# First V weights loaded into eight tiles of their own and split during the last rows of the start stage; one Sin for both rope tables

## The chip, the cores and the metric

The kernel runs on one core of one Trainium2 chip. The metric is the device time of one execution in microseconds. The kernel before was timed in 3 runs, with a median of 1419.71 us (1411.23 to 1421.71); a fourth execution was recorded by the hardware profiler.

## The reference, cut to what matters

One encoder layer on 1024 tokens of width 1024, float32. An adaLN vector gives shift and scale; `h` is the normed and modulated input; one projection of `h` gives, among others, the queries, keys and values of eight heads of banded attention ("chunk attention") and a rotary key of the latent attention.

```python
mod = jnp.dot(jax.nn.silu(c), w_ada[l]) + b_ada[l]
h = modulate(rmsnorm(x, g_attn_norm[l]), sh_a, sc_a)
proj = jnp.dot(h, w_in[l])
q_lat, kv_lat, k_rope, ca_qkv = jnp.split(proj, split_pts, axis=-1)
...
ang = positions.astype(jnp.float32)[..., None] * inv     # rope
cos = jnp.cos(ang)[:, :, None, :]
sin = jnp.sin(ang)[:, :, None, :]
```

Behind it come two attentions, an output projection, and a gated MLP with a short causal convolution.

## The kernel before

Tokens are tiled in 8 blocks of 128, the model width in 8 rows of 128 (`ND`, index `d`). Every product is made of three matmuls: each operand is split into a high half (rounded to the matmul's type) and a low half (the rest), and `gemm3` (lines 153 to 155) adds high by high (L153), high by low of the weight (L154) and low of the activation by high (L155). A weight tile is split in two steps: a copy that rounds (`hi_of`, L76 on ScalarE or L80 on VectorE) and a subtraction (`lo_of`, L83, mostly on POOL).

*The start stage* runs over `d` = 0 to 7. For each row, VectorE accumulates the adaLN vector from streamed weights (`adacc`, L254 and L256, tiles `adaw` in a ring of five), TensorE makes 8 transposes of `x` (`ht_ps`, L230), ScalarE and VectorE scale them (L233, L236, L238), POOL subtracts the low half of the first 512 tokens and VectorE that of the other 512 (both L239, tiles `hT`), and TensorE adds 24 matmuls to the first query/key product (`qk`).

*Behind the rows* the first V weights `wv0` are loaded by `load_w`: 8 tiles of 128 by 256 floats (128 KB each), in a ring of three raw tiles (`wr`) that all weights of this stage share. VectorE takes a sum of squares of each (L191, by `jt`) and rounds it (L80), POOL subtracts (L83). A block that is opened with `issue_after(x)` puts its instructions behind `x` on `x`'s engine; here the block stands behind the last low halves on VectorE and on POOL.

*Then the attention stage* begins. `f_v(0)` is the first of a list of "fillers": its products (`ipv`, 24 matmuls for 128 tokens) go through two PSUM banks (`mm`). 16 steps of the fillers, 96 matmuls, stand ahead of the first attention tile; then pages of queries and keys are transposed (`q_ps`, `k_ps`, L674) and score tiles (`sc`, L740) follow, with filler matmuls between them at a set ratio. `pow2_scale` (L298 to L310) makes a scale for V from the sums of squares, over one small matmul (`vspc`, L300). `qk_norm` norms queries and keys (L325 to L332, with a power on POOL, L117). The next weights, `wq1` and later `wq2`, come through the same ring `wr`; the bias tiles of the first heads (L852, masked on VectorE in L857 and L858) and all weights are issued by one queue, SyncE's (SP). The softmax is an Exp on ScalarE (L772) with a negative row minimum from VectorE (L761); its result is split (L72, L794) and transposed by DMA (L805).

The rope tables are a chain of small VectorE operations (`rope_tables`) that is woven into the attention stage; it ends with two Sin (L548 for the sine, L549 for the cosine), and four products each for two tables (L556). [...]

A scheduler puts each engine's instructions in order when the program is built, from the order in the source, the priorities and its own estimate of times; each engine then works through its list in that order.

Of the kernel before, what the change touches and what calls it, by code (L numbers as in the profile page):

```python
# [12 lines left out]
F32 = mybir.dt.float32  # L13
F32R = mybir.dt.float32r
# [3 lines left out]
AF = mybir.ActivationFunctionType  # L18
# [3 lines left out]
MUL, ADD, SUB, MIN, MAX = ALU.mult, ALU.add, ALU.subtract, ALU.min, ALU.max  # L22

P = 128
# [3 lines left out]
ND = D // P  # L28
# [35 lines left out]
def layer_kernel(ctx, tc, I, out):  # L64
    nc = tc.nc
    pe, act, dve, pool, sp = nc.tensor, nc.scalar, nc.vector, nc.gpsimd, nc.sync
# [7 lines left out]
    def hi_of(eng, o, i):  # L74
        if eng == "a":
            act.activation(o, i, AF.Copy)  # L76
        elif eng == "p":
            pool.tensor_scalar(o, i, 1.0, 0.0, op0=MUL, op1=ADD)
        else:
            dve.tensor_copy(o, i)  # L80

    def lo_of(eng, o, i, hi):
        (pool if eng == "p" else dve).tensor_tensor(o, i, f32(hi), op=SUB)  # L83
# [39 lines left out]
    hw = right.__enter__()  # L123
# [9 lines left out]
    st = startp.__enter__()  # L133
# [13 lines left out]
    anchor = {}  # L147
# [23 lines left out]
            yield 3 * len(part) * max(107, w / 2.4 + 2.5)  # L171


    def load_w(name, src, ncol, he="a", ssw=None, jt=None):
        tiles = []
        for k in range(ND):
            if ncol <= 256:
                w = hw.tile([P, 2, 256], F32R, name=f"{name}s{k}", tag="ws", bufs=16)
                hi, lo = w[:, 0, :ncol], w[:, 1, :ncol]
            else:  # L180
                wh = hw.tile([P, 512], F32R, name=f"{name}h{k}", tag="ws", bufs=16)
                wl = hw.tile([P, 512], F32R, name=f"{name}l{k}", tag="ws", bufs=16)
                hi, lo = wh[:, :ncol], wl[:, :ncol]
            for c0 in range(0, ncol, 256):
                c = slice(c0, min(c0 + 256, ncol))
                raw = hw.tile([P, 256], F32, name=f"{name}r{k}_{c0}", tag="wr", bufs=3)
                rw = raw[:, :c.stop - c0]
                anchor["sp"] = sp.dma_start(rw, src[:, k, c]).ins
                if jt:
                    junk = jt(f"{name}j{k}")[:, :c.stop - c0]  # L190
                    dve.tensor_tensor_reduce(junk, rw, rw, 1.0, 0.0, MUL, ADD, accum_out=ssw[:, k:k + 1])  # L191
                elif ssw is not None:
                    junk = qtile(f"{name}j{k}")
                    act.activation(junk[:, :c.stop - c0], rw, AF.Square, accum_out=ssw[:, k:k + 1])
                hi_of(he, hi[:, c], rw)
                lo_of("p", lo[:, c], rw, hi[:, c])
            tiles.append((hi, lo))
        return tiles
# [4 lines left out]

    def load_ada(dd, c):
        w = st.tile([P, 2, 512], F32, name=f"adaw_{dd}_{c}", tag="wa", bufs=5)
        sp.dma_start(w[:], I["w_ada_a"][dd][:, 2 * c:2 * c + 2])
        wada[dd, c] = w

    for c in range(4):
# [8 lines left out]
    for t in range(NT):  # L218
        xt = xs[t]
        junk = st.tile([P, D], mybir.dt.bfloat16, name=f"xj{t}", tag="hv", bufs=2)  # L220
# [25 lines left out]
    accs = {}  # L246
    ssw0 = cst.tile([P, ND], F32, name="ssw0")

    def ada_pair(dd):
        acc = rtile(f"adacc_{dd}")  # L250
        for k in range(ND):
            w = wada[dd, k // 2][:, k % 2]
            if k == 0:
                dve.tensor_scalar(acc[:], w, cs[:, 0:1], None, op0=MUL)  # L254
            else:
                dve.scalar_tensor_tensor(acc[:], w, cs[:, k:k + 1], acc[:], op0=MUL, op1=ADD)  # L256
        accs[dd] = acc

    ada_pair(0)
    for d in range(ND):  # L260
        dd, half = divmod(d, 2)
        if half == 0 and dd + 1 < ND // 2:
            for c in range(4):
                load_ada(dd + 1, c)
            ada_pair(dd + 1)
        pt = ps.tile([P, 512], F32, name=f"p_ada{d}", tag="mm", bufs=2)
        for i in range(2):
            c0 = half * 256 + i * P
            pe.matmul(pt[:, i:i + 1], accs[dd][:, c0:c0 + P], ones[:, 0:1], start=True, stop=True)

        tmp = cst.tile([P, 1], F32, name=f"adat{d}", tag="adat", bufs=2)
        dve.tensor_scalar(tmp[:], pt[:, 0:1], pk[:, C_B + 8 + d:C_B + 9 + d], 1.0, op0=ADD, op1=ADD)
        dve.tensor_tensor(modT[:, 0, d:d + 1], tmp[:], pk[:, C_GA + d:C_GA + d + 1], op=MUL)
        dve.tensor_tensor(modT[:, 1, d:d + 1], pt[:, 1:2], pk[:, C_B + d:C_B + d + 1], op=ADD)
        for h in range(2):
            hT[d, h] = mod_transpose(lambda j: xs[4 * h + j][:, d * P:(d + 1) * P], d, h, 0, ps, ("T", "pv")[h], 1,
                                     hw, "hT", st, 16, "v" if h else "a", "v" if h else "p")
        for t in range(NT):
            h, j = divmod(t, 4)
            sl = slice(j * P, (j + 1) * P)  # L280
            gemm3(qk0[h][:, j * 256:(j + 1) * 256],
                  [(hT[d, h][:, 0, sl], hT[d, h][:, 1, sl]) + wqk[d]], start=(d == 0 and j % 2 == 0), stop=(d == ND - 1 and j % 2 == 1))


    with tc.issue_after(anchor["lov"]), tc.issue_after(anchor["lop"]):
        wv0 = load_w("wv0_", I["w_v"][0], 256, he="v", ssw=ssw0,
                     jt=lambda n: st.tile([P, 512], F32, name=n, tag="hv", bufs=2))
    startp.__exit__(None, None, None)
    att = tc.tile_pool(name="att", bufs=1, side="left", reuse_waits="tile")
    at = att.__enter__()  # L290
# [192 lines left out]
    def rope_tables():  # L483
        cnt = [0]

        buf = [pgtile([P, 8, NT, 16], F32, f"rt{i}") for i in range(2)]

        def T():
            n = cnt[0] % 14
            cnt[0] += 1  # L490
            return buf[n // 8][:, n % 8]

        keep = (buf[1][:, 6], buf[1][:, 7])

        def rnd(src, q, o=None):
            o = T() if o is None else o
            dve.tensor_scalar(o, src, q, MAGIC, op0=MUL, op1=ADD)
            dve.tensor_scalar(o, o, MAGIC, None, op0=SUB)
            return o

        def fma(n, c, b):
            o = T()
            dve.scalar_tensor_tensor(o, n, c, b, op0=MUL, op1=ADD)
            return o

        p1 = _grid(TWO_PI, 2.0 ** -9)
        p2 = _grid(TWO_PI - p1, 2.0 ** -21)
        p3 = TWO_PI - p1 - p2

        def reduce(src):  # L510
            n = rnd(src, 1.0 / TWO_PI)
            yield
            r = fma(n, -p1, src)
            r = fma(n, -p2, r)
            yield
            return fma(n, -p3, r)

        pf = cst.tile([P, NT], F32, name="pf")
        dve.tensor_copy(pf[:], pos_i[:])
        ang = T()  # L520
        dve.tensor_tensor(ang, pf[:].unsqueeze(2).to_broadcast([P, NT, 16]),
                          pk[:, C_INV:C_INV + 16].unsqueeze(1).to_broadcast([P, NT, 16]), op=MUL)
        nh = rnd(ang, 2.0 ** -20, keep[0])
        rem = fma(nh, -(2.0 ** 20), ang)
        nm = rnd(rem, 2.0 ** -8, keep[1])
        lo = fma(nm, -(2.0 ** 8), rem)
        yield
        tot = yield from reduce(lo)
        for n, w in ((nh, 2.0 ** 20), (nm, 2.0 ** 8)):
            c = w - round(w / TWO_PI) * TWO_PI  # L530
            c1 = _grid(c, 2.0 ** -9)
            x = T()
            dve.tensor_scalar(x, n, c1, None, op0=MUL)
            yield
            x = fma(n, c - c1, (yield from reduce(x)))
            yield
            y = T()
            dve.tensor_tensor(y, tot, x, op=ADD)
            tot = y
        tot = yield from reduce(tot)  # L540
        yield
        pi_s = 3.1415925
        sn, cn, cl, c2, cl2 = T(), T(), T(), T(), T()
        dve.tensor_scalar(cl, tot, pi_s, -pi_s, op0=MIN, op1=MAX)
        dve.tensor_scalar(c2, tot, math.pi / 2, None, op0=ADD)
        yield
        dve.tensor_scalar(cl2, (yield from reduce(c2)), pi_s, -pi_s, op0=MIN, op1=MAX)
        act.activation(sn, cl, AF.Sin)  # L548
        act.activation(cn, cl2, AF.Sin)  # L549
        yield  # L550

        for tab, c0 in ((tabq, C_RQ), (tabk, C_RK)):
            for half, trig in ((0, cn), (1, sn)):
                for j in range(2):
                    o = half * 32 + j * 16
                    dve.tensor_tensor(tab[:, :, o:o + 16], trig,  # L556
                                      pk[:, c0 + j * 16:c0 + j * 16 + 16].unsqueeze(1)
                                      .to_broadcast([P, NT, 16]), op=MUL)
                    yield
# [285 lines left out]
    cnt = [0]  # L845
# [647 lines left out]
```

## Time and profile before

| | |
|---|---|
| runs | 1411.23, 1419.71, 1421.71 us; median 1419.71 |
| profiled execution | 1410.1 us; span of its trace 1408.3 us; mean granted TensorE clock 0.931 |
| busy in the span | TensorE 88%, VectorE 78%, POOL 50%, ScalarE 44% |
| chain that ended last | VectorE 35%, TensorE 30%, issue 10%, DMA 9%, POOL 8%, ScalarE 7% |

A row of the timeline gives start and duration in microseconds, the engine, the line, the operation, the tiles as out<-in, the count of merged instructions, and in brackets the idle time ahead of it with what ended it. A row of a group gives, after the bar, busy time and the mean nanoseconds of one. A row of waits gives total, number and longest. A row of the table by stretches gives for each engine busy microseconds and instructions, then the granted clock, the share of the DMA engines and GB/s. PE is TensorE, PEld its weight loads, DVE VectorE, ACT ScalarE, SPq the queue of SyncE.

### The profile page before, as it was taken

To read this page: it belongs to the slowest core of one execution; us is meant where nothing else is said; L and a number is where in the kernel's file an instruction comes from. 1 tells how busy PE (TensorE), PEld (TensorE's weight loads), DVE (VectorE), ACT (ScalarE), POOL (GpSimd) and SP (SyncE) were. 2 spreads that over 40 slices of the span, in tenths; PEclk is the share of its full clock that TensorE was granted. 3 is DMA by queue.
4 is the path that set the end of the run, shared out by engine and by line. 5 is a ranking of instruction groups with operands and counts; after the bars stand their busy time and mean duration, and the time that the engine had idled before them with its cause. 6 is when DMAs were issued, how large, how long until landed. Compare 5 with 4: busy or idle time off the path is not lost.

```text
span 1408.3 us, 18699 instructions
## 1 busy us (share of the span) xinstructions
PE 1234.5 (88%) x6156; PEld 1006.3 (71%) x6156; DVE 1093.0 (78%) x1861; ACT 624.0 (44%) x1132; POOL 709.3 (50%) x685
## 2 busy tenths in 40 slices
PE   4879688989777789995677999999999999999998
PEld 3868476978655567774565887787778777888886
DVE  6847879686579997882577888988888888698667
ACT  4433545444456554652274444344434444443331
POOL 5353366375545674443563677677667874200000
PEclk9989798998888889997887999999999999999999
DMA  8223567755221478877721323333232223894451
GB/s 314 93 64 79 132 149 177 169 134 106 57 53 42 88 169 178 164 160 230 279 90 45 113 95 123 127 119 127 91 108 89 101 99 118 303 350 130 125 163 60
DMA packets 223689, 190.56 MB, mean 135 GB/s; under 512 B 148709, under 2 KB 166885, under 8 KB 223593
## 3 DMA queue, kind: packets, MB, share of 16 engines
q1 hardware_dynamic: 223592, 189.38, 47.3%
q8 instruction: 48, 0.79, 0.2%
q14 instruction: 49, 0.39, 0.1%
HBM read 117.24 MB, written 37.49 MB: 110 GB/s over the span
## 4 chain that ended last, share of the span: by engine, by line
DVE 35%; PE 30%; issue 10%; DMA 9%; POOL 8%; ACT 7%; SPq 1%; POOLq 0%; DVEq 0%; ACTq 0%
DVE u L1157 5%; DVE u L1156 4%; PE dnA_P L1304 2%; PE dnA_P L1305 2%; PE dnA_P L1306 2%; ACT u L1155 2%; DVE hlc L794 2%; PE dnB_P L1306 1%; PE dnB_P L1305 1%; PE dnB_P L1304 1%; DVE hlm L794 1%; DMA wor<-w_out 1%; DMA aw<-w_ada 1%; PE sc L740 1%; PE sm L746 1%
## 5 line engine op out<-in xcount | busy, mean ns | idle before, releaser
L76 ACT ACTIVATE dnP<-dnr 128x1024 fp32r<-128x1024 f32 x73 | 77.3, 1062 | 111.8 <-PE dnA_P L1306 43.1
L1278 DVE TENSOR_TENSOR dnP<-dnr,dnP 128x1024 fp32r<-128x1024 f32 x72 | 90.3, 1259 | 44.9 <-ACT dnP L76 43.3
L1156 DVE SCALAR_TENSOR_TENSOR u<-c,cvp,u 128x1023 f32<-128x1023 f32 x44 | 81.9, 1902 | 46.3 <-ACT u L1155 46.3
L72 POOL TENSOR_SCALAR hlm<-Pm,rim 128x512 f16<-128x512 f32 (+2 forms) x96 | 69.8, 736 | 71.8 <-DVE rim L775 28.7
L1157 DVE SCALAR_TENSOR_TENSOR u<-c,cvp,u 128x1022 f32<-128x1022 f32 x44 | 86.5, 2003 | 0.0
L72 POOL TENSOR_SCALAR hlc<-Pc,ric 128x640 f16<-128x640 f32 (+2 forms) x64 | 47.1, 738 | 71.1 <-DVE ric L775 35.4
L794 DVE SCALAR_TENSOR_TENSOR hlm<-Pm,rim,hlm 128x512 f16<-128x512 f32 (+2 forms) x96 | 65.0, 688 | 6.2 <-POOL hlm L72 5.9
L772 ACT ACTIVATE Pc<-sc,mc 128x640 f32<-128x640 f32 (+2 forms) x64 | 42.1, 658 | 54.5 <-DVE mc L761 38.9
L772 ACT ACTIVATE Pm<-sm,mm 128x128 f32<-128x128 f32 (+3 forms) x64 | 47.1, 737 | 32.0 <-DVE mm L765 18.6
L794 DVE SCALAR_TENSOR_TENSOR hlc<-Pc,ric,hlc 128x640 f16<-128x640 f32 (+2 forms) x64 | 53.0, 830 | 10.0 <-POOL hlc L72 9.3
L76 ACT ACTIVATE wc<-ws 128x512 fp32r<-128x512 f32 x22 | 13.9, 633 | 103.1 <-DVE ws L1082 103.1
L1155 ACT ACTIVATE u<-c,cvp 128x1024 f32<-128x1024 f32 x44 | 52.1, 1234 | 13.5 <-DVE c L1228 6.8
L153 PE MATMUL ipq<-wq_s,hT 128*128 128x256 f32 x192 | 56.2, 296 | 1.2 <-ACT wq_s L76 1.2
L154 PE MATMUL ipq<-wq_s,hT 128*128 128x256 f32 x192 | 56.0, 292 | 0.6 <-POOL wq_s L83 0.6
L155 PE MATMUL ipq<-wq_s,hT 128*128 128x256 f32 x192 | 56.1, 292 | 0.0
L833 PE MATMUL pvm<-PTm,vt 128*128 128x256 f16 (+1 forms) x320 | 43.2, 284 | 12.6 <-DMA PTm<-hlm 8.8
L1232 ACT ACTIVATE u<-u 128x1024 f32<-128x1024 f32 x22 | 23.3, 1061 | 67.9 <-DVE u L1157 67.9
L83 POOL TENSOR_TENSOR wc<-ws,wc 128x512 fp32r<-128x512 f32 x22 | 34.3, 1558 | 36.4 <-ACT wc L76 36.4
L1306 PE MATMUL dnA_P<-dnP 128*128 128x512 f32 x132 | 51.4, 389 | 0.0
L1305 PE MATMUL dnA_P<-dnP 128*128 128x512 f32 x132 | 51.4, 389 | 0.0
L1304 PE MATMUL dnA_P<-dnP 128*128 128x512 f32 x132 | 51.2, 389 | 0.0
L83 POOL TENSOR_TENSOR wd<-wu,wd 128x512 fp32r<-128x512 f32 x22 | 30.4, 1382 | 37.5 <-ACT wd L76 37.5
(421 smaller groups left out, 4544.6 us busy)
## 6 DMA issues: line engine op xcount, KB each, us to landing
wu<-w_up SPq DMA_DIRECT2D x44, 512.0 KB, 3.5
dnr<-g_d SPq DMA_DIRECT2D x73, 256.0 KB, 4.3
aw<-w_ada SPq DMA_DIRECT2D x48, 256.0 KB, 3.5
g_d<-u SPq DMA_DIRECT2D x22, 512.0 KB, 2.8
dnr<-w_down SPq DMA_DIRECT2D x44, 256.0 KB, 5.4
adaw<-w_ada_a SPq DMA_DIRECT2D x16, 512.0 KB, 4.9
x<-x SPq DMA_DIRECT2D x16, 512.0 KB, 8.5
g_d<-gs SPq DMA_DIRECT2D x22, 256.0 KB, 2.0
```

What stands on the lines that cost most here:

```text
L72: pool.tensor_scalar(o, i, s, 1.0, op0=MUL, op1=MUL)
L76: act.activation(o, i, AF.Copy)
L83: (pool if eng == "p" else dve).tensor_tensor(o, i, f32(hi), op=SUB)
L772: act.activation(pr[:, :n], sv, AF.Exp, bias=m[:], scale=-1.0, accum_out=rsum[:, 0:1])
L794: dve.scalar_tensor_tensor(hl[:, w:2 * w], pp, ri[:], hl[:, :w], op0=MUL, op1=SUB)
L1155: act.activation(u[:], c, AF.Identity, scale=cvp[:, cv + 2:cv + 3], bias=cvp[:, cv + 3:cv + 4])
L1156: dve.scalar_tensor_tensor(u[:, 1:], c[:, :S - 1], cvp[:, cv + 1:cv + 2], u[:, 1:], op0=MUL, op1=ADD)
L1157: dve.scalar_tensor_tensor(u[:, 2:], c[:, :S - 2], cvp[:, cv:cv + 1], u[:, 2:], op0=MUL, op1=ADD)
L1278: r = f(*a, **k)
L1304: pe.matmul(pt, sh, w[:, 0, 0], start=start, stop=False, skip_group_check=add)
L1305: pe.matmul(pt, sh, w[:, 1, 0], start=False, stop=False, skip_group_check=add)
L1306: pe.matmul(pt, sl, w[:, 0, 0], start=False, stop=stop, skip_group_check=add)
```

## The change

First, `wv0` no longer goes through `load_w`. Eight raw tiles of their own (`wvr`, 8 buffers) are loaded right behind the last `adaw` load on SyncE's queue. They are split two at a time behind the low halves of rows 4, 5, 6 and 7: VectorE rounds and then sums squares, POOL subtracts. Second, the two Sin become one over 256 columns, whose two inputs lie side by side; the ring of small tiles in the chain shrinks from 14 to 10 for that.

```diff
-    def load_w(name, src, ncol, he="a", ssw=None, jt=None):
+    def load_w(name, src, ncol, he="a", ssw=None):
...
-                if jt:
-                    junk = jt(f"{name}j{k}")[:, :c.stop - c0]
-                    dve.tensor_tensor_reduce(junk, rw, rw, 1.0, 0.0, MUL, ADD, accum_out=ssw[:, k:k + 1])
-                elif ssw is not None:
+                if ssw is not None:
...
-        sp.dma_start(w[:], I["w_ada_a"][dd][:, 2 * c:2 * c + 2])
+        anchor["ada"] = sp.dma_start(w[:], I["w_ada_a"][dd][:, 2 * c:2 * c + 2]).ins
...
+    wv0, wv0r = [], []
+
+    def wv0_load():
+        with tc.issue_after(anchor["ada"]):
+            for k in range(ND):
+                r = st.tile([P, 256], F32, name=f"wv0_r{k}", tag="wvr", bufs=8)
+                anchor["sp"] = sp.dma_start(r[:], I["w_v"][0][:, k, :]).ins
+                wv0r.append(r)
+
+    def wv0_split(k):
+        w = hw.tile([P, 2, 256], F32R, name=f"wv0_s{k}", tag="ws", bufs=16)
+        junk = st.tile([P, 512], F32, name=f"wv0_j{k}", tag="wvj", bufs=1)
+        with tc.issue_after(anchor["lov"]), tc.issue_after(anchor["lop"]):
+            hi_of("v", w[:, 0], wv0r[k][:])
+            lo_of("p", w[:, 1], wv0r[k][:], w[:, 0])
+            dve.tensor_tensor_reduce(junk[:, :256], wv0r[k][:], wv0r[k][:], 1.0, 0.0, MUL, ADD,
+                                     accum_out=ssw0[:, k:k + 1])
+        wv0.append((w[:, 0], w[:, 1]))
...
             for c in range(4):
                 load_ada(dd + 1, c)
+            if dd + 2 == ND // 2:
+                wv0_load()
             ada_pair(dd + 1)
...
+        if d >= ND // 2:
+            for k in range(2 * d - ND, 2 * d - ND + 2):
+                wv0_split(k)
         for t in range(NT):
...
-    with tc.issue_after(anchor["lov"]), tc.issue_after(anchor["lop"]):
-        wv0 = load_w("wv0_", I["w_v"][0], 256, he="v", ssw=ssw0,
-                     jt=lambda n: st.tile([P, 512], F32, name=n, tag="hv", bufs=2))
...
-            n = cnt[0] % 14
+            n = cnt[0] % 10
...
-        sn, cn, cl, c2, cl2 = T(), T(), T(), T(), T()
+        cl, cl2, sn, cn, c2 = buf[1][:, 2], buf[1][:, 3], buf[1][:, 4], buf[1][:, 5], T()
...
-        act.activation(sn, cl, AF.Sin)
-        act.activation(cn, cl2, AF.Sin)
+        act.activation(buf[1][:, 4:6], buf[1][:, 2:4], AF.Sin)
```

## The prediction

> **What bounds the kernel now.** I read the table by stretches first, then the waits, then the queue and the engines in the stretch that stands out. The page says TensorE is 88% busy in a span of 1408.3 us, but the share is uneven.
>
> ```profile
> 56.00:68.00 12.00, 12.00 (x103) 11.99 (x103) 7.45 (x21) 6.30 (x10) 3.43 (x5) 1.00 0.01 2
> 68.00:93.20 25.20, 17.47 (x100) 15.49 (x99) 12.43 (x42) 6.72 (x15) 19.74 (x25) 0.73 0.28 86
> 101.20:140.00 38.80, 37.63 (x276) 33.64 (x277) 28.91 (x102) 17.28 (x38) 12.90 (x18) 1.00 0.32 72
> ```
>
> The last rows of the start stage fill TensorE (12.00 of 12.00 us). Then come 25.2 us with only 100 matmuls at a granted clock of 0.73, and after 101.2 TensorE is full again (37.63 of 38.80). The hole is the first V product.
>
> ```profile
> PE ipv L154 <- POOL wv_s L83: 4.2, 3, 3.5
> PE ipv L153 <- DVE wv_s L80: 1.5, 1, 1.5
> PE vspc L300 <- DVE vsc L298: 1.4, 1, 1.4
> ```
> ```profile
> SPq L188 <- POOL wv_s L83: 30.8, 4, 21.6
> ```
> ```profile
> 39.20 1.92 SPq L206 DMA_DIRECT2D adaw<-w_ada_a  x2
> 43.59 33.73 SPq L188 DMA_DIRECT2D wv_r<-w_v  x7
> 77.37 0.90 SPq L852 DMA_DIRECT2D bias<-bias  x2
> 78.37 15.33 SPq L188 DMA_DIRECT2D wq_r<-w_qk  x11
> ```
>
> TensorE waits for both halves of the V weights. The cause is the ring of three raw tiles: SyncE stands 21.6 us in one wait until POOL has released a tile, so seven loads of 128 KB take 33.73 us, and the biases and `wq1` queue behind them. TensorE's own rows give the pace:
>
> ```profile
> 65.19 0.40 PE L155 MATMUL qk<-wq_s,hT 128*128 128x256 f32 x2
> 68.00 0.28 PE L153 MATMUL ipv<-wv_s,hT 128*128 128x256 f32 x1
> 71.73 0.39 PE L153 MATMUL ipv<-wv_s,hT 128*128 128x256 f32 x1 [1.52 <-DVE wv_s L80]
> 75.61 0.58 PE L154 MATMUL ipv<-wv_s,hT 128*128 128x256 f32 x1 [3.49 <-POOL wv_s L83]
> 80.79 0.59 PE L300 MATMUL vspc<-vsc,ones 128*128 128x8 f32 x2 [1.41 <-DVE vsc L298]
> 81.82 0.58 PE L153 MATMUL ipv<-wv_s,hT 128*128 128x256 f32 x1 [0.43 <-DVE vsc L301]
> 93.00 0.28 PE L154 MATMUL ipv<-wv_s,hT 128*128 128x256 f32 x1
> 93.12 0.28 PE L155 MATMUL ipv<-wv_s,hT 128*128 128x256 f32 x1
> 101.20 0.30 PE L740 MATMUL sc<-k,qh 128*128 128x128 f32 x1 [1.64 <-DVE k L705]
> ```
>
> The 96 matmuls run from 68.00 to 93.24. Undisturbed they start every 0.12 us (the rows at 93.00 and 93.12), 11.5 us in all. The first score follows the last of them by 8 us.
>
> **The change part by part.** *The wait for V's weights.* With eight tiles nothing holds the loads back. The row at 39.20 shows the last `adaw` issued by 41.1; the queue row at 77.37 has 0.45 us for each 128 KB issue, so eight take 3.6 us and two biases 0.9, issued by 46. The first split stands behind row 4's low half, after 55, so the loads are hidden by 9 us of other work. The stretch of 25.2 us becomes 11.5 plus the handover at `vspc` (80.79 to 81.82, 1.0 us), which stays because it holds a PSUM bank of the pair. Gain: 25.2 - 12.5 = 12.7 us.
>
> *The splits, moved.* They now share rows 4 to 7 with work that TensorE waits for.
>
> ```profile
> 54.79 1.30 POOL L239 TENSOR_TENSOR hT<-hv,hT 128x512 fp32r<-128x512 f32 x1 [1.08 <-ACT hv L236]
> 62.76 1.32 POOL L239 TENSOR_TENSOR hT<-hv,hT 128x512 fp32r<-128x512 f32 x1 [2.42 <-ACT hv L236]
> ```
> ```profile
> 55.01 1.62 DVE L239 TENSOR_TENSOR hT<-hv,hT 128x512 fp32r<-128x512 f32 x1
> 61.38 0.81 DVE L238 TENSOR_SCALAR hv<-ht_ps,modT 128x512 f32<-128x512 f32 x1 [2.20 <-ACT hT L233]
> 62.22 0.69 DVE L239 TENSOR_TENSOR hT<-hv,hT 128x512 fp32r<-128x512 f32 x1
> ```
> ```profile
> L83 POOL TENSOR_TENSOR wv_s<-wv_r,wv_s 128x256 fp32r<-128x256 f32 x8 | 6.6, 846 | 3.4 <-DVE wv_s L80 3.2
> L117 POOL TENSOR_TENSOR r<-ss,nhalf 128x8 f32<-128x8 f32 x4 | 6.5, 1642 | 0.1
> L83 POOL TENSOR_TENSOR wq_s<-wq_r,wq_s 128x256 fp32r<-128x256 f32 x8 | 5.9, 734 | 3.7 <-ACT wq_s L76 3.7
> L191 DVE CUSTOM_DVE_ANT_0 wv_j<-wv_r 128x256 f32<-128x256 f32 x8 | 4.3, 548 | 3.0 <-DMA wv_r<-w_v 3.0
> L80 DVE CAST wv_s<-wv_r 128x256 fp32r<-128x256 f32 x8 | 2.7, 355 | 0.0
> L857 DVE TENSOR_SCALAR bias<-bias,pk 128x256 f32<-128x256 f32 x2 | 0.7, 346 | 0.0
> ```
>
> VectorE gets 2 x (0.36 + 0.55) = 1.8 us in a row and has 2.2 idle (61.38): it fits. POOL is tighter. In the built program its list has the subtractions of tiles 3, 4 and 5 ahead of row 7's low half, and tiles 4 and 5 are rounded on VectorE only behind row 6's low half there, which ended at 62.22 + 0.69 = 62.9. Round, square, round (0.36 + 0.55 + 0.36), then 0.73 on POOL: row 7's low half starts at 64.9 instead of 62.76, 2.1 late. It ended at 64.1 and TensorE used it at about 65.3 (second of the two at 65.19), so 1.2 us cover it and 0.9 shows. Row 6 has the same shape: 0.9 again. I take 2.0 with a little for the engines slowing each other. Bounds: 0 if idle time holds all, and 8 x 0.73 = 5.9 if every subtraction shows.
>
> [...] The row at 55.01 shows VectorE's subtraction at 1.62 us while POOL subtracts, against 0.69 alone. [...]
>
> *Bias masks.* VectorE's list has both masks (2 x 0.35, and two small fills) ahead of row 4's scaling, so 0.7 us or a little more is added there, and if the biases landed late VectorE would stand. They are issued by 46 and needed after 51. Behind VectorE wait the last `adacc` and TensorE's `p_ada`. I take 0.4; bounds 0 and 0.9.
>
> *The second ring.* What is late next is `wq1`, still in three tiles.
>
> ```profile
> 92.11 0.42 ACT L76 ACTIVATE wq_s<-wq_r 128x256 fp32r<-128x256 f32 x1 [1.07 <-DMA wq_r<-w_qk]
> 92.43 0.46 ACT L371 ACTIVATE v<-ipv,vabc 128x256 f16<-128x256 f32 x1
> ```
> ```profile
> 89.57 2.51 DMA wq_r<-w_qk
> 154.40 1.28 ACT L772
> 168.04 1.28 ACT L772
> 181.16 4.41 DMA wq_r<-w_qk
> 186.96 3.37 DMA aw<-w_ada
> ```
>
> The chain ran through this ring up to 92, just as TensorE finished: ScalarE evicts V behind the last `wq1` split. The new list on ScalarE has V's evictions between the splits of tiles 4, 5, 6 and 7, and POOL reaches `wq1` about 12 us earlier, behind three of the 1.64 us powers. One trip of the ring is 2.51 + 0.42 + 0.73 = 3.7 us. TensorE would finish near 82.9; I reckon two trips after POOL's third `wq1` subtraction near 79, so it is close: I take 0.5, bounds 0 and one trip, 3.7.
>
> *The Sin.* Two set loads and one Sin go.
>
> ```profile
> 150.81 1.28 ACT L548 ACT_TABLE_LOAD   x1
> 152.11 0.31 ACT L548 ACTIVATE rt<-rt 128x128 f32<-128x128 f32 x1
> ```
>
> The load ahead of Exp at 154.40 stands on the chain with 1.28 us; the one at 150.81 is covered by VectorE. I take -1.3; bounds 0 and -2.6 (both loads). [...]
>
> *The order behind it.* The scheduler also moved things in the lists from about 105 to 600 us, with the same instructions. No row prices that. The nearest are the two transfers on the chain at 181.16 and 186.96, 7.8 us, where weights stood behind other transfers on SyncE. I take 0 and 7.8 to either side.
>
> Sum: -12.7 + 2.0 + 0.4 + 0.5 - 1.3 + 0 = **-11.1 us**. Against the profiled execution's own 1410.1 that is 1399.0; against the median of the runs, 1419.71, it is 1408.6. The four executions form two pairs ten microseconds apart (1410.1 and 1411.2; 1419.7 and 1421.7), and a median of a few can fall into either, so I set the saving against their mean, 1415.7: **1404.6 us**.
>
> **The rivals.** *The ring takes the wait.* V's evictions wait on ScalarE for two more trips of `wq1` (7.4 us): -12.7 + 2.4 + 7.4 - 1.3 = -4.2, 1411.5. For it: the chain runs through just this ring now. Against it: the lists interleave. *The ports.* Every one of the eight VectorE squares meets a POOL subtraction and each meeting costs the 0.93 us of row 55.01, 7.4 in place of 2.0: -5.7, 1410.0. Against it: VectorE has 2.2 us idle in a row. *The new order helps.* `wq2`'s fourth to sixth tile are now issued in one go on SyncE; if the 7.8 us of the chain at 181 to 190 go, -18.9, 1396.8. *The new order hurts, and it ends slower.* Place: SyncE's list, where weights now stand ahead of the softmax transposes that TensorE's value products need; while a weight waits for its ring, the transposes behind it stand. Price: 7.8 us each time, as above. One such leaves -3.3; from the second on the kernel is slower (-11.1 + 15.6 = +4.5, 1420.2), and three give +12.3, 1428.0. Against it: POOL's list has the subtractions that free those tiles early. *The change doesn't do what it says:* biases or weights land late and VectorE stands in row 4; about 0, 1415.
>
> **How the numbers follow.** Forecast 0.52, order helps 0.17, ring 0.11, ports 0.08, order hurts 0.09, no effect 0.03. The extremes of all bounds are -12.7 - 2.6 - 7.8 = -23.1 (1392.6) and -12.7 + 5.9 + 0.9 + 3.7 + 7.8 = +5.6 (1421.3); runs in one pair or the other move this by some 5 us. The range is 1391 to 1422. One per cent, 14.2 us, is about what a measurement of this kernel can tell from no change. Faster by more than that: most of "order helps" and a quarter of the forecast case, 0.28. Slower by more: half of "order hurts" and a little of the unknown, 0.08. Within: 0.64.
>
> **What would show it.** Right: eight V loads issued between 41 and 46; no wait of TensorE on `wv_s`; about 13 us instead of 25.2 from the first `ipv` to the 96th, at a clock near 1.00; the first score near 91; one Sin of 256 columns with two set loads around it. Row 6 or 7 wrong: TensorE waits for POOL's `hT` by more than 2 us in all. Ring: ScalarE's V copies stand behind `wq_s` waiting for DMA and the first score is after 95. Order: the gain at 101.2 shrinks or grows between 105 and 600. The prediction is wrong if the first score comes early and the end does not.

## The result, and the profile after

The changed kernel takes 1406.3 us (median of 20 runs, 1399.0 to 1412.2) against 1414.45 us of the kernel before (20 runs, 1408.14 to 1427.44). The ratio is 0.9941, 95% interval 0.9925 to 0.9958; by the ratio that is 8.3 us less. Run again beside the later experiments it gave 0.9941 once more (0.9922 to 0.9961). The profiled execution after, 1412.2 us, is the longest of its runs, and the one before, 1410.1, is among the shortest of its own; so the two traces are compared stage by stage and not by their ends, and each kernel has a second trace (after 1404.9 us, before 1415.2).

The table by stretches of the first trace after (columns as in the prediction's):

```profile
56.00:68.00 12.00, 11.17 (x90) 10.31 (x88) 11.93 (x32) 5.13 (x7) 6.86 (x8) 1.00 0.01 2
68.00:93.20 25.20, 20.57 (x148) 20.27 (x149) 14.45 (x31) 9.54 (x22) 18.82 (x23) 0.87 0.14 43
```

The hole has shrunk: 148 matmuls instead of 100 in the same 25.2 us, at a clock of 0.87 instead of 0.73. The price stands in the row above it: in the last rows of the start stage TensorE is no longer full (11.17 of 12.00, 90 matmuls instead of 103) and VectorE now is (11.93).

SyncE's queue and its longest wait:

```profile
41.50 6.49 SPq L252 DMA_DIRECT2D wv_r<-w_v  x8
48.04 0.91 SPq L869 DMA_DIRECT2D bias<-bias  x2
```
```profile
SPq L188 <- POOL wq_s L83: 37.0, 8, 27.1
```

The eight loads are out by 48 and the biases by 49. The long wait on a ring of three now belongs to `wq1`. TensorE's waits between 50 and 95 us have no `wv_s` among them any more:

```profile
PE ipv L153 <- DVE v L390: 3.0, 1, 3.0
PE qk L155 <- POOL hT L236: 2.2, 2, 1.5
PE qk L155 <- DVE hT L236: 0.6, 1, 0.6
```

TensorE's own rows give the new pace:

```profile
71.89 0.28 PE L153 MATMUL ipv<-wv_s,hT 128*128 128x256 f32 x1
84.05 0.60 PE L691 MATMUL q_ps<-ident,qn 128*128 128x128 f32 x4
87.62 0.55 PE L153 MATMUL ipv<-wv_s,hT 128*128 128x256 f32 x1 [2.97 <-DVE v L390]
94.62 0.60 PE L691 MATMUL k_ps<-ident,qn 128*128 128x128 f32 x4
96.86 0.30 PE L757 MATMUL sc<-k,qh 128*128 128x128 f32 x1 [1.64 <-DVE k L722]
```

The first V product starts 3.9 us later than before (71.89, before 68.00), the 96 matmuls take 12.2 us (25.2), and from there to the first score pass 12.8 us (8.0). So the first score gains 4.3 us in this trace; in the second one it comes at 93.67. The prediction had it near 91.

*Why the rows are later.* VectorE in rows 4 to 7, and then POOL in rows 6 and 7:

```profile
55.55 1.39 DVE L80 CAST wv_s<-wv_r 128x256 fp32r<-128x256 f32 x1
...
59.77 0.14 DVE L291 TENSOR_TENSOR modT<-adat,pk 128x1 f32<-128x1 f32 x1
...
60.63 0.28 DVE L80 CAST wv_s<-wv_r 128x256 fp32r<-128x256 f32 x1
...
61.92 1.26 DVE L291 TENSOR_TENSOR modT<-adat,pk 128x1 f32<-128x1 f32 x1
63.18 0.97 DVE L261 CUSTOM_DVE_ANT_0 wv_j<-wv_r 128x256 f32<-128x256 f32 x1
68.28 1.62 DVE L236 TENSOR_TENSOR hT<-hv,hT 128x512 fp32r<-128x512 f32 x1
```
```profile
55.35 1.43 POOL L236 TENSOR_TENSOR hT<-hv,hT 128x512 fp32r<-128x512 f32 x1 [0.89 <-ACT hv L233]
61.81 1.35 POOL L236 TENSOR_TENSOR hT<-hv,hT 128x512 fp32r<-128x512 f32 x1
68.06 1.28 POOL L236 TENSOR_TENSOR hT<-hv,hT 128x512 fp32r<-128x512 f32 x1
```

An operation of 128 by 1 takes 1.26 us while POOL subtracts (61.92) and 0.14 two microseconds earlier (59.77); a cast 1.39 or 0.28. Each long one ends where POOL's subtraction beside it ends or just behind: 63.18 against 63.16 (61.81 + 1.35), 56.94 against 56.78 (55.35 + 1.43). The low halves of rows 6 and 7 start at 61.81 and 68.06 on POOL; row 7's stood at 62.76 before.

*Why the first score is later behind the V product.* POOL, VectorE and ScalarE near 82:

```profile
76.98 3.25 POOL L117 TENSOR_TENSOR r<-ss,nhalf 128x8 f32<-128x8 f32 x2
80.19 0.73 POOL L83 TENSOR_TENSOR wq_s<-wq_r,wq_s 128x256 fp32r<-128x256 f32 x1
82.31 0.56 POOL L321 TENSOR_TENSOR vsc<-vsc,nhalf 128x1 f32<-128x1 f32 x1
```
```profile
82.90 0.15 DVE L323 TENSOR_SCALAR vsc<-vsc 128x1 int32<-128x1 int32 x1 [1.42 <-POOL vsc L321]
...
83.17 0.14 DVE L327 TENSOR_SCALAR vabc<-vsc 128x1 f32<-128x1 f32 x1
```
```profile
83.38 0.42 ACT L76 ACTIVATE wq_s<-wq_r 128x256 fp32r<-128x256 f32 x1 [3.47 <-DMA wq_r<-w_qk]
83.70 0.46 ACT L389 ACTIVATE v<-ipv,vabc 128x256 f16<-128x256 f32 x1
```

V's evictions need the scale, and the scale needs a power on POOL (82.31) that stands behind three powers of the query norm and the `wq1` subtractions. On ScalarE the first eviction (83.70) stands besides behind a `wq1` split that has waited 3.47 us for its tile. The scale is ready at 83.31 (83.17 + 0.14), and the copy follows the split at 83.70: the two holds end within 0.4 us of each other, and the split is the last.

### The profile page after: what moved, and what is told of

It reads as the page before. It is cut to its first block, busy times and chain, and to the rows that moved or that the text cites. A ratio compares the mean times of both kernels' runs of the same rounds, so it can differ in the third digit from the quotient of the medians.

```text
span 1410.4 us, 18704 instructions
## 1 busy us (share of the span) xinstructions
PE 1237.9 (88%) x6156; PEld 1012.0 (72%) x6156; DVE 1099.7 (78%) x1861; ACT 620.9 (44%) x1129; POOL 712.9 (51%) x685
## 4 chain that ended last, share of the span: by engine, by line
DVE 21%; PE 17%; POOL 6%; issue 6%; ACT 4%; DMA 2%; SPq 0%; DVEq 0%; POOLq 0%; ACTq 0%
DVE u L1174 5%; DVE u L1173 4%; PE dnA_P L1321 2%; PE dnA_P L1322 2%; PE dnA_P L1323 2%; ACT u L1172 2%; PE dnB_P L1322 1%; PE dnB_P L1321 1%; PE dnB_P L1323 1%; DVE u L1250 1%; DVE c L1245 1%; DVE gmbc L1160 1%; DVE wu L1102 1%; DVE wu L1101 1%; DVE ws L1099 1%
## 5 line engine op out<-in xcount | busy, mean ns | idle before, releaser
L72 POOL TENSOR_SCALAR hlm<-Pm,rim 128x512 f16<-128x512 f32 (+3 forms) x96 | 68.7, 724 | 85.2 <-DVE rim L792 21.6
L811 DVE SCALAR_TENSOR_TENSOR hlm<-Pm,rim,hlm 128x512 f16<-128x512 f32 (+3 forms) x96 | 67.7, 715 | 8.6 <-POOL hlm L72 8.1
L850 PE MATMUL pvm<-PTm,vt 128*128 128x256 f16 (+1 forms) x320 | 47.0, 295 | 30.3 <-DMA PTm<-hlm 29.7
L850 PEld LDWEIGHTS <-vt 128*128 128x128 f16 x320 | 31.2, 108 | 46.8 <-issue 22.2
L76 ACT ACTIVATE wc<-ws 128x512 fp32r<-128x512 f32 x22 | 13.9, 633 | 103.0 <-DVE ws L1099 103.0
L153 PE MATMUL ipq<-wq_s,hT 128*128 128x256 f32 x192 | 57.4, 301 | 1.2 <-ACT wq_s L76 1.2
L154 PE MATMUL ipq<-wq_s,hT 128*128 128x256 f32 x192 | 57.7, 301 | 0.1
L155 PE MATMUL ipq<-wq_s,hT 128*128 128x256 f32 x192 | 57.3, 299 | 0.0
L1249 ACT ACTIVATE u<-u 128x1024 f32<-128x1024 f32 x22 | 23.3, 1061 | 71.1 <-DVE u L1174 71.0
```

The lines of the kernel that those rows point to most:

```text
L72: pool.tensor_scalar(o, i, s, 1.0, op0=MUL, op1=MUL)
L811: dve.scalar_tensor_tensor(hl[:, w:2 * w], pp, ri[:], hl[:, :w], op0=MUL, op1=SUB)
L850: last = pe.matmul(dst, u.vst(j), mov, start=(x == 0), stop=(x == len(todo) - 1), skip_group_check=True)
```

## The experiments

All edits are on the changed kernel if nothing else is said. "First V" and "first score" are the starts of these matmuls in the profiled execution; "wait" is TensorE's wait for the transposed softmax tiles (PTm) in latent attention.

| kernel | first V | first score | wait | median us | ratio to before |
|---|---|---|---|---|---|
| before, two traces | 68.0, 69.9 | 101.2, 103.0 | 8.8, 8.9 | 1414 to 1417 | 1 |
| after, two traces | 71.9, 71.3 | 96.9, 93.7 | 29.7, 24.6 | 1406.3, 1407.1 | 0.9941 |
| V part alone, two traces | 72.1, 72.0 | 95.9, 95.9 | 17.0, 17.0 | 1418.0 | 1.0019 |
| Sin alone | 68.2 | 101.2 | 18.6 | 1414.7 | 1.0004 |
| splits behind row 7 | 68.3 | 97.0 | 17.1 | 1413.4 | 0.9991 |
| scale first | 71.1 | 89.7 | 19.2 | 1397.8 | 0.9886 |
| scale first, own `wq1` tiles | 73.0 | 92.7 | 25.9 | 1408.3 | 0.9945 |
| subtraction on VectorE | 70.1 | 90.9 | 25.3 | 1404.3 | 0.9921 |
| rounding on ScalarE | 70.5 | 93.9 | 20.8 | 1403.3 | 0.9909 |
| scale first + VectorE | 71.0 | 89.9 | 28.2 | 1407.9 | 0.9957 |
| scale first + ScalarE | 70.9 | 89.5 | 19.3 | 1399.9 | 0.9895 |

**The V part alone** keeps the two Sin and their ring of 14.

```diff
...
-        act.activation(buf[1][:, 4:6], buf[1][:, 2:4], AF.Sin)
+        act.activation(sn, cl, AF.Sin)
+        act.activation(cn, cl2, AF.Sin)
```

> Only the V part of the change; the two Sin and their ring of 14 stay as before. Theory (sum of terms at the first score: the V wait gives 13.1 us, rows 4 to 7 cost 3.9, V's evictions behind POOL's powers and the second ring cost 4.9, so 4.3 us are left, and the Sin adds the rest later): first score near 96.9, total 4 to 5 us under before, ratio near 0.997. Rival (the new order of the lists behind 105 us, not the Sin, gives the rest): 8 us under before, ratio near 0.994.

Measured: 1418.03 us, ratio 1.0019 (0.9997 to 1.0041). Neither theory came out: the first score gains 5.3 us, and nothing of it is left at the end. **The Sin alone** is that part on the kernel before.

> Only the one Sin over 256 columns with the ring of 10; V's weights as before. Theory: first score unchanged at 101.2; one set load with its Sin leaves the chain, 1.3 to 3.5 us under before, ratio 0.9975 to 0.999. Rival (the loads were hidden and the rest of the gain belongs to V): ratio 1.000 within 0.1%.

Measured: 1414.68 us, ratio 1.0004 (0.9982 to 1.0026): the rival's time, though the gain doesn't belong to the V part alone either. At its own place the edit does more than was counted. TensorE's waits around the two Sin before, and around the one in the second trace after:

```profile
156.63 0.90 PE L740 MATMUL sc<-k,qh 128*128 128x256 f32 x2 [2.01 <-ACT Pc L772]
163.28 2.31 PE L833 MATMUL pvc<-PTc,v 128*128 128x256 f16 x12 [3.04 <-DMA PTc<-hlc]
170.28 0.39 PE L740 MATMUL sc<-k,qh 128*128 128x256 f32 x1 [2.04 <-ACT Pc L772]
```
```profile
147.63 0.90 PE L757 MATMUL sc<-k,qh 128*128 128x256 f32 x2 [0.45 <-ACT Pc L789]
152.74 2.31 PE L850 MATMUL pvc<-PTc,v 128*128 128x256 f16 x12 [1.49 <-DMA PTc<-hlc]
158.72 0.33 PE L757 MATMUL sc<-k,qh 128*128 128x128 f32 x1 [1.37 <-ACT Pc L789]
```

These three add to 7.1 us before and to 3.3 after, and to the same 3.3 with the Sin alone (0.45, 1.46, 1.37). That is 3.8 us less there, and the time of the kernel with the Sin alone does not show it. The two parts give nothing alone and 8.3 us together, so they are not two terms that add up: what follows behind 105 us differs from kernel to kernel.

**All splits behind the last row.**

```diff
-        if d >= ND // 2:
-            for k in range(2 * d - ND, 2 * d - ND + 2):
-                wv0_split(k)
...
+    for k in range(ND):
+        wv0_split(k)
```

> The whole change, but all eight splits stand behind the last row instead of two by two behind rows 4 to 7; the loads stay early. Theory (the splits in the rows cost 3.9 us through POOL and VectorE holding each other up): the first V matmul is back near 68 to 69, but then POOL gives a tile every 0.75 to 0.85 us against 0.36 us of matmuls, 3 to 4 us of waits, so the 96th ends near 84 as with the change and the total is within 2 us of it. Rival (the place of the splits matters: rows are the dear place): the 96th ends near 81 and the total is 3 us under the change.

Measured: 1413.36 us, ratio 0.9991 (0.9966 to 1.0016). The first V product starts where it did before:

```profile
68.28 0.28 PE L153 MATMUL ipv<-wv_s,hT 128*128 128x256 f32 x1
```

So the early loads and the bias masks cost the rows at most 0.3 us, and the splits in the rows the 3.0 to 3.6 us between this row and the two traces after. The V stretch is longer in exchange (18.6 us), and the first score is as late as in the first trace after. Neither sign came: the 96th product ends at 87.0 and not near 84 or 81, and the time is some 7 us over the change's and not within 2 of it or under it.

**V's scale ahead of the first V product.**

```diff
+            if t == 0 and pp == 0:
+                vscale["c", pp] = pow2_scale(f"c{pp}", ssw[:], hb[:], ND, 2.0 * D)
+                sc = vscale["c", pp][0]
             yield from proj2(pt, t, w, 256)
-            if t == 0:
+            if t == 0 and pp:
```

> The whole change, and V's scale (the small matmul over the sums of squares and its chain) is made ahead of the first V product instead of behind its first 48 matmuls. Theory (V's evictions wait for POOL's power for the scale, which stands behind two powers and three subtractions): scale ready near 76 instead of 83.3, TensorE's wait of 3.0 us ahead of the third V product gone, its clock kept, first score near 93 to 94, 3 us under the change, ratio to before near 0.992. Rival (the second ring of three holds the evictions, not the scale): the scale is ready early but V's copies still stand behind weight splits that wait for DMA, first score within 1 us of 96.9.

Measured: 1397.84 us, ratio 0.9886 (0.985 to 0.9923), the best of all. TensorE's waits between 68 and 95 us, whole view:

```profile
PE sc L760 <- DVE k L725: 1.6, 1, 1.6
PE qk L155 <- POOL hT L236: 1.5, 1, 1.5
```
```profile
77.18 0.47 ACT L392 ACTIVATE v<-ipv,vabc 128x256 f16<-128x256 f32 x1 [2.19 <-PE ipv L155]
82.39 0.42 ACT L76 ACTIVATE wq_s<-wq_r 128x256 fp32r<-128x256 f32 x1 [3.12 <-DMA wq_r<-w_qk]
```

The wait for V's eviction is gone, though `wq1` still comes through its ring of three, and the first score follows the 96th matmul by 7.0 us. The edit took both holds away at once: the power runs at 71.76, and with the scale early the scheduler put V's first two copies (77.18 and 78.81) ahead of the split that waits for the ring (82.39), where the changed kernel had them behind it. So it doesn't show which of the two held the eviction.

**The same with `wq1` in the eight raw tiles that V leaves**, loaded in one go. For that the tile pool of the attention stage is opened behind these loads; two lines of the edit:

```diff
+            r = st.tile([P, 256], F32, name=f"wq1_r{k}", tag="wvr", bufs=8)
+            anchor["sp"] = sp.dma_start(r[:], I["w_qk"][1][:, k, :]).ins
...
```

> Two edits on the changed kernel: V's scale is computed ahead of the first V product, and wq1 is loaded in one go into the eight raw tiles that V's weights leave. Its lists behind the start are the changed kernel's own, so the gain at the first score should arrive at the end. Theory (the scale's power behind other work on POOL costs 4.8 us, the ring of three costs what the ScalarE waits for wq_r show): first score 89 to 90 by the scale alone, 86 to 88 if the ring still held V's evictions; time 1406.3 - 7 to 10 = 1396 to 1399. Rival (what the start gains is given back behind 105 us, as in the kernel with all splits behind the last row): first score as early, but time 1402 or more.

Measured: 1408.32 us, ratio 0.9945 (0.9924 to 0.9966). First score at 92.7 and not 86 to 88: with the scale early, taking the ring away gains nothing more, though 1.9 of the 3.0 us by which this first score is later than that of "scale first" are there at the first V product already (73.0 against 71.1). `wq1`'s own tiles without the early scale were not run; how long the scale alone would have held the evictions stays open. The time fits the rival: the earlier first score did not arrive at the end.

**The subtractions on VectorE**, and **the rounding on ScalarE**:

```diff
-            lo_of("p", w[:, 1], wv0r[k][:], w[:, 0])
+            lo_of("v", w[:, 1], wv0r[k][:], w[:, 0])
```

> One edit on the changed kernel: the eight subtractions of V's splits are done by VectorE instead of POOL. First V product at 71.9 in the changed kernel, 68.0 in the kernel before. Theory A (rows 6 and 7 are late since POOL's own low halves stand behind the V subtractions and VectorE and POOL slow each other): POOL's hT of row 7 comes back to about 63 to 65, VectorE's casts and squares return to 0.3 and 0.5 us, and the first V product starts at 68 to 70. Theory B (the rows are late since VectorE has no room for the splits): VectorE gets 8 x 0.69 = 5.5 us more, and the first V product starts at 73 or later. The time follows the first score by the same amount: by A 1403 to 1406, by B 1408 to 1412.

```diff
-            hi_of("v", w[:, 0], wv0r[k][:])
+            hi_of("a", w[:, 0], wv0r[k][:])
```

> One edit on the changed kernel: V's weights are rounded by ScalarE instead of VectorE (8 x 0.36 = 2.9 us less on VectorE by its uncontended rows, up to 8 us by the contended ones). If VectorE's load makes rows 6 and 7 late, the first V product falls from 71.9 to about 69.5 to 70.5; if it is POOL's list, it stays at 71 to 72. The scale's power stays where it is on POOL, so the first score follows within 1 us of 96.9 less whatever the rows gain. The lists behind the start differ here, so the end can move by up to 8 us to either side for that alone.

Measured: 1404.28 us (0.9921, 0.9895 to 0.9948) and 1403.33 us (0.9909, 0.9878 to 0.994). Groups of VectorE between 40 and 72 us, first after, then with the subtractions on VectorE (busy us and mean ns behind the bar):

```profile
L80 DVE CAST wv_s<-wv_r 128x256 fp32r<-128x256 f32 x8 | 5.5, 690 | 0.0
L236 DVE TENSOR_TENSOR hT<-hv,hT 128x512 fp32r<-128x512 f32 x6 | 5.0, 828 | 0.1
```
```profile
L80 DVE CAST wv_s<-wv_r 128x256 fp32r<-128x256 f32 x8 | 4.5, 562 | 0.0
L236 DVE TENSOR_TENSOR hT<-hv,hT 128x512 fp32r<-128x512 f32 x6 | 4.0, 674 | 0.0
L83 DVE TENSOR_TENSOR wv_s<-wv_r,wv_s 128x256 fp32r<-128x256 f32 x8 | 3.3, 416 | 0.0
```

VectorE has eight instructions more to do, and the first V product still starts 1.2 to 1.8 us earlier: theory B falls, and A misses its 70 by 0.1. POOL's `hT` of row 7 starts at 64.03, as A said, but the casts come back to 562 ns in the mean and not to 300: two of the eight take 1.38 and 1.40 us beside a subtraction of POOL's `hT`, the others 0.28. VectorE's own operations are faster without these eight subtractions on POOL beside them (the casts 562 ns in the mean against 690, the `hT` subtractions 674 against 828), and it does a subtraction in 416 ns where POOL took 831. With the rounding on ScalarE the first V product comes to 70.5, as was expected if VectorE's load makes the rows late, though the sums of squares now take the stretch in the casts' place (895 ns in the mean, 555 in the changed kernel). So both count: VectorE has no idle time left in these rows (11.93 of 12.00 us busy), and what it does beside POOL's subtractions takes longer; at 0.28 us each, the eight casts would take 2.2 us instead of 5.5.

The first score with the rounding on ScalarE misses its expectation (96.9 less the 1.4 us gained in the rows, within 1): at 93.9 it is 3.0 us earlier than in the first trace after, and 0.2 later than in the second. Its trace also parts the two holds on V's evictions: the scale is ready at 81.85, and the first copy of V starts at 82.93 only, right behind a `wq1` split (82.60) that waited 0.96 us for its tile. There the ring held them 1.1 us longer than the scale.

**A second trace of the changed kernel.**

> The changed kernel once more, for a second trace of the same lists. In its first trace TensorE waited 29.7 us in latent attention for the transposed softmax tiles (PTm), against 8.8 before and 17 to 19 in four other kernels, and the stretch from the end of banded attention to the output projection took 260.8 us against 251.3. If this comes from the order of the lists (theory), the second trace shows 25 us or more of this wait and 259 us or more for the stretch again. If it changes from run to run (rival), the wait falls to 10 to 20 us and the stretch to 250 to 256. The start repeats in both: first V product near 71.9, first score near 96.9. Time 1406, within 3.

Measured: 1407.14 us; this trace 1404.9. The latent wait is 24.6 us (25 or more was the theory's, 10 to 20 the rival's) and its stretch 259.9 (260.8 in the first): nearer to the theory, so it comes with the lists in the main. The start didn't repeat as expected: the first score is at 93.67 and not near 96.9. What did change is the clock. The table by stretches, first trace, then second:

```profile
88.00:92.00 4.00, 4.00 (x20) 4.00 (x20) 1.16 (x3) 1.01 (x2) 1.71 (x3) 0.50 0.26 81
```
```profile
88.00:92.00 4.00, 4.00 (x34) 3.79 (x33) 0.69 (x1) 0.54 (x2) 1.34 (x2) 1.00 0.20 68
```

And the second trace's rows beside those at 87.62 and 96.86:

```profile
87.05 0.36 PE L153 MATMUL ipv<-wv_s,hT 128*128 128x256 f32 x1 [2.98 <-DVE v L390]
93.67 0.30 PE L757 MATMUL sc<-k,qh 128*128 128x128 f32 x1 [1.64 <-DVE k L722]
```

The same list and the same wait (2.97 and 2.98 us): once TensorE does the matmuls behind it at a granted clock of 0.50 and once at 1.00, and the way from 87 to the first score takes 9.2 or 6.6 us. What decides between the two, the traces don't show: from the end of the last product to the next it is 3.4 us in both (84.22 to 87.62 and 83.63 to 87.05), with four transposes of 0.60 us in all at its start. The kernel with the rounding on ScalarE has 3.0 us between the two products, and its clock is 0.50 from 86 to 88 us:

```profile
85.87 0.55 PE L153 MATMUL ipv<-wv_s,hT 128*128 128x256 f32 x1 [2.57 <-DVE v L390]
```

**Second traces of the kernel before and of the V part alone.**

> The kernel before, for a second trace of the same lists. Theory (what is lost behind the start lies in the order of the lists): latent attention repeats, TensorE's wait for PTm is 8 to 12 us again (8.8 in the first trace; 17 to 30 in all nine other kernels and traces) and the stretch from the last product of banded attention to the output projection 250 to 254 us (251.3; 257 to 268 in the others). Rival (chance of one run): a wait of 17 us or more and 257 us or more. The start repeats in both: first V product at 68.0, the 96th at 93, first score at 101.2, with TensorE's clock at 0.50 while it waits for V's weights.

> The V part alone once more, for a second trace. In its first one the first score came 5.3 us earlier than before (95.9) and nothing of it was left at the end (1418.3 us of span), with a granted clock of 0.72 between 140 and 200 us. If lists and the two separate Sin do it, the second trace loses the same in the same places: waits of TensorE of 2.0, 3.2 and 2.0 us around the two Sin between 154 and 170 us, and a latent stretch of 260 us or more. If half of it was the clock's luck in one run, the span falls below 1412 and the clock between 140 and 200 us rises above 0.80.

Measured: 1415.15 and 1416.9 us. The latent waits repeat to 0.1 us:

```profile
PE pvm L833 <- DMA PTm<-hlm: 8.9, 6, 5.3
```
```profile
PE pvm L851 <- DMA PTm<-hlm: 17.0, 9, 3.9
```

The V part alone waits 2.01, 3.22 and 1.95 us around its two Sin again, has the clock of 0.72 between 140 and 200 us again, and 262.2 us for the latent stretch (262.4): the theory of lists and Sin holds there. For the kernel before, the wait repeats but the stretch does not (257.1, first 251.3): the rival's length with the theory's wait, so the wait alone doesn't set that stretch. Its first V product came at 69.9 and not 68.0, and the table by stretches says why, first trace and second:

```profile
48.00:52.00 4.00, 3.46 (x29) 3.23 (x28) 3.96 (x12) 1.47 (x3) 0.00 (x0) 1.00 0.00 0
```
```profile
48.00:52.00 4.00, 4.00 (x20) 4.00 (x20) 3.96 (x12) 1.23 (x2) 0.00 (x0) 0.50 0.02 6
```

**Both gains together.**

> Two edits on the changed kernel together: V's scale ahead of the first V product, and the subtractions of V's splits on VectorE. Alone they brought the first score to 89.7 and 90.9 and the time to 1397.8 and 1404.3. If the two costs are separate terms, the first V product starts near 70 and the first score comes at 87.5 to 88.5, and the time is 1395 to 1397. If the lists decide, the first score is as early and the time is 1400 or more.

> Two edits on the changed kernel together: V's scale ahead of the first V product, and V's weights rounded by ScalarE. Alone they brought the first V product to 71.1 and 70.5, the first score to 89.7 and 93.9, the time to 1397.8 and 1403.3. If the two costs are separate terms, the first V product starts at 70 to 70.5, the first score comes at 88.5 to 89.5 and the time is 1394 to 1398. If the lists decide, the time is 1400 or more at as early a first score.

Measured: 1407.88 us (0.9957, 0.9934 to 0.9981) and 1399.88 us (0.9895, 0.9856 to 0.9935). The first scores come at 89.9 and 89.5, like "scale first" alone (89.7): the terms of rows and scale don't add. The second lies a little outside what was expected of separate terms (70.9, 89.5 and 1399.9). The first is the clearest case for the lists. Until 290 us it stands with "scale first" to 0.2 us (first block of the next stage at 289.6 and 289.8) and ends 10 us later in the median (0.7% by the two ratios). Latent attention, "scale first" and then with the subtractions on VectorE:

```profile
PE pvm L853 <- DMA PTm<-hlm: 19.2, 9, 4.9
```
```profile
PE pvm L853 <- DMA PTm<-hlm: 28.2, 16, 4.8
```

Nine microseconds more of one wait, far from any edit.

## Why the prediction was right or wrong, point by point

The forecast was 1404.6 us, within 1% and a little faster; it came out at 1406.3. The sign was right, the saving was 8.3 us of the forecast's 11.1, and the main mechanism was right at its own place: the wait for V's weights is gone by the forecast amount. That the end came so near is partly luck. Several terms were wrong and cancelled, the two parts give nothing alone, and the first score, forecast near 91, came at 96.9 and 93.7. The baseline of 1415.7 was near the 1414.45 of 20 runs, but those do not fall into the two pairs that the prediction saw in four.

| term | predicted us (bounds) | measured us |
|---|---|---|
| wait for V's weights | -12.7 | -12.3 to -13.0 (25.2, 24.4 to 12.2, 12.2) |
| splits in rows 4 to 7 | +2.0 (0 to 5.9) | +3.0 to +3.6 against the splits behind row 7 |
| bias masks | +0.4 (0 to 0.9) | at most 0.3 |
| second ring | +0.5 (0 to 3.7) | +1.6 to +4.8 (8.0, 8.6 to 10.2, 12.8) |
| Sin | -1.3 (-2.6 to 0) | -3.8 in TensorE's waits there, nothing in the time of the edit alone |
| order of the lists | 0 (-7.8 to 7.8) | up to 10 between two kernels with the same first score |

*The wait for V's weights* was right: its cause, its size and the signs named for it. SyncE took 6.5 us and not 3.6 for the eight loads, which the cover of 9 us swallowed.

*The splits*: the step "it fits" on VectorE failed. It added the means of the kernel before (0.36 and 0.55); the squares kept theirs (555 ns), but the casts took 690 ns in the mean beside POOL. That was the rival called the ports: right that VectorE is slower beside POOL (a cast took 1.39 us there and 0.28 alone), though no run shows what the two engines share; wrong in that the squares would pay and not the casts, too dear in its price of 7.4, and the idle time on VectorE paid for a part. The sign for rows 6 and 7, a wait of more than 2 us for POOL's `hT`, came true with 2.2.

*The second ring* was mis-sized, and its working left out a second hold of the same length. The sign of the ring rival appeared in the first trace: V's evictions behind a `wq_s` that waits for its load, and a first score after 95. The working counted trips of the ring and not the scale, though it mentions that POOL reaches `wq1` behind three of the 1.64 us powers. The scale's own power stands behind them too, and the two holds ended within 0.4 us of each other. The edit that made the scale early removed both; taking the ring away besides gained nothing. The 4.8 us of the first trace, above the bound, are the wait and then the clock of 0.50 behind it; without that it is 1.6 against the second trace before.

*The Sin* was taken at one set load. The trace before has four set loads around the two Sin (ACT_TABLE_LOAD, 1.28 us each), one ahead of each Sin (150.81, 166.42) and one ahead of the next Exp (154.40, 168.04); the second trace after has two (151.71, 156.49). TensorE's waits for the Exp and for the transposes of its result fell by 3.8 us there, more than the 2.6 of both loads.

*The order* got no value, and the uncertainty was put at one weight transfer. "The prediction is wrong if the first score comes early and the end does not" happened with the V part alone, not with the whole change. The rival "order hurts" named weights ahead of the softmax transposes on SyncE. A longer wait for these transposes did come (8.8 to 29.7 and 24.6 us), but SyncE's own waits between 400 and 660 us, before and then after, show VectorE's softmax split as the largest (TensorE's wait in the first trace after, then SyncE's):

```profile
PE pvm L850 <- DMA PTm<-hlm: 29.7, 17, 4.8
```
```profile
SPq L805 <- DVE hlm L794: 29.9, 18, 10.4
```
```profile
SPq L822 <- DVE hlm L811: 44.6, 27, 10.3
```

So the transposes were late on what VectorE does first, and the named place was not shown. Which part of the 8.3 us is owed to the edits and which to the lists stays open: every edit changes the lists too, and no run here holds them fixed.

## What to carry to other kernels

Give the first weights of a new stage their own tiles when a ring holds their loads back, but cost the work that moves along by its durations beside the other engine and not alone (VectorE's casts here: 0.28 us alone, 0.69 in the mean in these rows). When one wait goes, follow every input of the next instruction and what stands ahead of it in its engine's list: here a scale of one column on a busy POOL and a weight split on ScalarE were late next, and computing the scale 10 us earlier, with the order that the scheduler then chose, brought the first score forward by 4 to 7 us. A part that gives nothing alone can still be needed for a gain: judge an edit at its own place in the trace, and don't take differences of some 10 us at the end for the edit's as long as a scheduler writes new lists each time.

## What the runs showed of the hardware that was not expected

Behind the same wait of TensorE (2.97 and 2.98 us) one trace lost another 2.6 us: the granted clock stood at 0.50 for some 6 us of matmuls in it and at 1.00 in the other. The kernel before has the same between 48 and 52 us (0.50 against 1.00, 20 matmuls against 29), behind waits that are alike in both traces (1.2 us at 40 and 0.7 at 43), and its first V product moved by 1.9 us. So single traces of one kernel differed here by 1.9 to 2.6 us with the clock; what sets it, they don't show.

VectorE's slowing beside POOL did not go by size: an operation of 128 by 1 went from 0.14 to 1.26 us, a cast of 128 by 256 from 0.28 to 1.39, a subtraction of 128 by 512 from 0.69 to 1.62. It went by what was left of POOL's operation. All ten operations of VectorE that are lengthened between 55 and 72 us in the first trace after began during one of POOL's subtractions and end 0.02 to 0.56 us behind it, by about their own length less 0.13: the subtraction of 68.28 ends at 69.90, 0.56 behind POOL's (68.06 + 1.28). None of the ten was done before POOL was. A sum of squares that began 0.16 us ahead of POOL kept its 0.41 us (60.83, POOL's at 60.99), and a scaling from PSUM kept its 0.80 beside one (67.44, POOL's from 67.25 to 68.11). So in these ten meetings the price was the rest of POOL's operation less some 0.13 us, and the one square that had begun ahead of POOL paid nothing.
